# A second array of expert sums that takes odd ranks up to 57 and is read back by accumulating DMAs

## The chip, the core and the metric

The kernel runs on one core of a Trainium2 chip. Its time is the device time of one execution in microseconds (us); the median of several runs is compared. The core has five engines with a queue of instructions each: TensorE (PE, with its weight loads listed apart as PEld), VectorE (DVE), ScalarE (ACT), GpSimd (POOL) and SyncE (SP), which only issues DMAs here. DMAs are carried by 16 DMA engines that all queues share.

## What is computed

One layer of a decoder for 520 tokens (512 of a prompt, 8 samples): a mixer of a state-space branch and dilated attention, a layer norm, and then a mixture of 64 experts, of which each token takes 8. The change touches only the end of the mixture:

```
x  = layer_norm(alpha*x + mixer(x))
acc = zeros(n+1, D);  for each block of tokens of one expert e:
    h  = silu(x[tok] @ w1[e]) * (x[tok] @ w3[e])
    acc[tok] += (h @ w2[e]) * gate
ff  = acc + shared_expert(x)
ple = sigmoid(x @ w_ple_gate) * (p @ w_ple)
x   = layer_norm(alpha*x + ff + ple)
```

All weights are fp32. Every matmul is done as three products of high and low parts.

## The kernel before

After the mixer, `second_phase` norms the residual `x1` (104 tokens on partitions, five tiles of 1024), routes the tokens and sorts the experts by how many tokens they have. The place in that order is the expert's rank, 0 to 63; `CAPS` is the number of rows of each rank, falling from 112 to 56. A loop over `e` from 0 to 64 then works through them: `expert_in(e)` (two products with w1 and w3), `turn(e + 1)` (transposes of the next rank's rows), `expert_out(e - 1)` (the product with w2), `fetch(e + 3)` (token indices of a later rank and the gather of its rows from DRAM on GpSimd's queue). Six weight chunks of 512 KB a rank are loaded by SP and split into high and low parts by ScalarE with VectorE, or with GpSimd for one chunk of six (`lo` at line 265).

`expert_out` scales its rows on ScalarE into `y` (line 1450, two buffers, `YB = 2`) and adds them to a DRAM array of sums with an indirect accumulating DMA, the scatter of line 1451, issued from GpSimd. There are two such arrays, `sumsD[0]` and `sumsD[1]`, zeroed early (line 426). Ranks below `SECOND` = 50 alternate between them; ranks 50 to 61 all go to array 0. Two accumulating DMAs into one array must not overlap, so a scatter waits until the one before it in the same array has landed; GpSimd takes its queue in order and stands while it waits. Also `y` of a rank waits for the landing of the scatter two before, whose buffer it takes. Ranks 62 and 63 do not scatter: their rows stay on chip (`kept`, `last_rows`) and are added by matmuls in `last_norm`.

Beside the experts the loop takes side products from a list: 36 items of the shared expert and of the layer inputs, three that bring the scales of the last norm, and in the kernel before five `second_sums(i)`. An item is due when `(e - 4) * SIDE` reaches its number in the list. `second_sums(i)` loads a tile of array 1 on SP's queue into a buffer (`second`, line 1375) and adds it to `x1[:, i]` on GpSimd (line 1376, recorded at the helper's line 262). After the loop, SP loads the five tiles of array 0 (`acc`, line 1637), GpSimd adds three of them to `x1`, and `last_norm` does the rest: `total(i)` adds the kept rows by matmuls (line 1738 on VectorE), then the norm and the output. A conditional `overflow` (line 1645), not taken here, lies ahead of it.

The order of instructions on each engine is not that of the text: a planner simulates the program at build time, and issues on each engine what is ready in its own simulation, the earlier in the text first.

Of the kernel before, what the change touches and what calls it, by code (L numbers as in the profile page):

```python
# [18 lines left out]
F32 = mybir.dt.float32  # L19
# [4 lines left out]
ALU = mybir.AluOpType  # L24
# [6 lines left out]
TT = 104  # L31
# [16 lines left out]
YB = 2  # L48
PRE = 5
VB = 5  # L50
N_SIDE = 44
SECOND = 50
SIDE = N_SIDE / 55
N_DENSE = 54
assert len(CAPS) == NE

# [144 lines left out]
def trunk_step(ctx: ExitStack, tc: tile.TileContext, I, O):  # L201
    nc = tc.nc
    V, S, G = nc.vector, nc.scalar, nc.gpsimd
# [27 lines left out]
    def open_pool(*a, **k):  # L231
        cm = pool(*a, **k)
        p = cm.__enter__()
        opened.append((p, cm))
        return p

    def close_pool(p):
        at = next(n for n, (q, _) in enumerate(opened) if q is p)
        opened.pop(at)[1].__exit__(None, None, None)
# [21 lines left out]
    def add(e, o, a, b):  # L261
        return e.tensor_tensor(out=o, in0=a, in1=b, op=ALU.add)
# [85 lines left out]
    H, EX = {}, {}  # L348
# [68 lines left out]
    sumsD = [dram.tile([640, 1024], F32, name=f"accD{n}") for n in range(2)]  # L417
# [319 lines left out]
    side = []  # L737
# [357 lines left out]
    R5 = range(5)  # L1095
# [162 lines left out]
    def ffn_turn(hg, m):  # L1258
        ps = bank()
        for k in range(2):  # L1260
            T.transpose(ps[:, m * k:m * k + m], hg[0:m, 128 * k:128 * k + 128], ident[0:m, 0:m])
        hh, hl = (moe.tile([128, 2, MAX_CAP], F32R, tag=nm, bufs=2, name=nm)[:, :, 0:m] for nm in ("hh", "hl"))
        H['turned'] = split(hh, hl, ps[:, 0:2 * m].rearrange("p (k t) -> p k t", k=2))
        return hh, hl
# [9 lines left out]
    def shared_mid(out, hg):  # L1274
        S.activation(hg, out[:, 0:128], AF.Silu)
        mul(V, hg, hg, out[:, 128:256])
        return hg

    def shared_turn(hg, i, c):

        ps = bank()
        T.transpose(ps[:, 0:TT], hg, ident[0:TT, 0:TT])
        split(H['shared'][:, i, 0, c], H['shared'][:, i, 1, c], ps[:, 0:TT])
# [87 lines left out]

    def second_sums(i):

        t = pw.tile([128, 1024], F32, tag="praw", name="second")[0:TT]
        nc.sync.dma_start(t, sumsD[1][TT * i:TT * i + TT])
        add(G, H['x1'][:, i], H['x1'][:, i], t)


    XG, XT, HG, HT, GC, IX = {}, {}, {}, {}, {}, {}
# [3 lines left out]
    def find(e, what=(0, 1)):  # L1383

        m = CAPS[e]
        if e not in OH:
            OH[e] = one_hot(e, m)
        a, b = what[0], what[-1] + 1
        ps = psx.tile([128, 512], F32, tag="x", name="x") if e > 2 else bank()
        for i in R5:  # L1390
            T.matmul(ps[0:m, 3 * a:3 * b], lhsT=OH[e][:, i], rhs=H['what'][:, i, 3 * a:3 * b, e], start=(i == 0), stop=(i == 4))
        both = moe.tile([128, 2], F32, tag="gc", bufs=8, name="both")
        V.tensor_reduce(both[0:m, a:b], ps[0:m, 3 * a:3 * b].rearrange("p (w n) -> p w n", n=3), axis=AX.X, op=ALU.add)
        if 0 in what:
            IX[e] = moe.tile([128, 1], I32, tag="idx", bufs=8, name="idx")
            H['last'] = V.tensor_scalar(IX[e][0:m], both[0:m, 0:1], 1024.0, H['slots'][0:m], op0=ALU.add, op1=ALU.min)  # L1396
        if 1 in what:
            GC[e] = both[:, 1:2]
            if e < NE - 2:
                OH.pop(e)  # L1400
# [7 lines left out]
    def fetch(e):  # L1408
        find(e)
        gather(e)  # L1410

    def gather(e):
        m = CAPS[e]
        G.indirect_dma_start(out=XG[e % 3][0:m], out_offset=None, in_=xD[:, :],  # L1414
                             in_offset=bass.IndirectOffsetOnAxis(ap=IX[e][0:m, 0:1], axis=0),
                             bounds_check=NT - 1, oob_is_err=False)

    def turn(e):
        x, m = XG[e % 3], CAPS[e]
        XT[e] = [moe.tile([128, 8, MAX_CAP], F32R, tag=nm, bufs=2, name=nm)[:, :, 0:m] for nm in ("xgh", "xgl")]  # L1420
        for z in range(2):
            ps = bank()
            for j in range(4):
                k = 4 * z + j
                T.transpose(ps[:, m * j:m * j + m], x[0:m, 128 * k:128 * k + 128], ident[0:m, 0:m])
            src = ps[:, 0:4 * m].rearrange("p (k t) -> p k t", k=4)
            split(XT[e][0][:, 4 * z:4 * z + 4], XT[e][1][:, 4 * z:4 * z + 4], src)

    def expert_in(e):
        ps, m = bank(), CAPS[e]  # L1430
        for q in range(4):
            hi, lo = (t.rearrange("p (k n) -> p k n", k=2) for t in stream.get(AT[e] + q))
            ffn_in(ps[0:m], *XT[e], hi, lo, q, slice(0, m))
        HG[e] = ffn_mid(ps, m)
        XT.pop(e)

    def expert_out(e):
        ps, m = mm2(), CAPS[e]
        hh, hl = HT.pop(e)
        for k in range(2):  # L1440
            hi, lo = stream.get(BT[e] + k)
            for n, (l, w) in enumerate(((hh, hi), (hh, lo), (hl, hi))):
                for h in range(2):
                    T.matmul(ps[0:m, h], lhsT=l[:, k], rhs=w[:, 512 * h:512 * h + 512], start=(k == 0 and n == 0),
                             stop=(k == 1 and n == 2))
        if e >= NE - 2:
            kept(e, ps)
            return
        y = py.tile([MAX_CAP, 1024], F32, tag="y", bufs=YB, name="y")[0:m]
        S.activation(y.rearrange("p (h n) -> p h n", h=2), ps[0:m], AF.Copy, scale=GC.pop(e)[0:m])  # L1450
        G.indirect_dma_start(out=sumsD[e % 2 if e < SECOND else 0][:, :], out_offset=bass.IndirectOffsetOnAxis(ap=IX.pop(e)[0:m, 0:1], axis=0),  # L1451
                             in_=y, in_offset=None, compute_op=ALU.add)
# [24 lines left out]
    def second_phase():  # L1477
# [9 lines left out]
        x1 = H['x1']  # L1487
# [107 lines left out]
        close_pool(disp)  # L1595
        py = open_pool("py")
        side = [(q, i) for q in range(-2, 4) for i in range(-1, 5)]
        side += [(4, -1), (4, 0), (4, 1)] + [(5, i) for i in R5]
        for e in range(NE + 1):
            if e == NE - 1:  # L1600
                last_rows()
            if 0 < e < NE:
                expert_in(e)
            if 0 < e < NE - 1:
                turn(e + 1)
            if e:
                expert_out(e - 1)
            else:
                H['shared'] = py.tile([128, 5, 2, 2, TT], F32R, tag="side", name="st")
                mids = py.tile([MAX_CAP, 1024], F32, tag="y", bufs=YB, name="mids")  # L1610
                mids = [shared_mid(H['first half'][i], mids[0:TT, 128 * i:128 * i + 128]) for i in R5]
            if 0 < e < 6:
                shared_turn(mids[e - 1], e - 1, 0)
            if 0 < e < NE - 1:
                HT[e] = ffn_turn(HG.pop(e), CAPS[e])
            if e + 3 < NE:
                fetch(e + 3)
            if e == 4:
                close_pool(pre)
                pw = open_pool("pw")  # L1620
            while side and (e - 4) * SIDE >= N_SIDE - len(side) + 1:
                q, i = side.pop(0)
                if q == -2:
                    shared_more(i)
                elif q == -1:
                    shared_out(i)
                elif q < 4:
                    layer_inputs(q, i)
                elif q == 5:
                    second_sums(i)  # L1630
                else:
                    last_scales(i)
        assert not side
# [65 lines left out]
    def last_rows():  # L1699

        yy = pw.tile([128, 2, 1024], F32R, tag="pl", name="yy")
        H['yh'], H['yl'] = yy[:, 0], yy[:, 1]
        to = H['to'] = pw.tile([128, 5, TT], F32R, tag="praw", name="to")
        G.memset(yy.bitcast(F32), 0.0)
        G.memset(to.bitcast(F32), 0.0)
        for e in (NE - 2, NE - 1):
            m, z = CAPS[e], 64 * (NE - 1 - e)
            oh = OH.pop(e)
            for tiles in ((0, 1, 2), (3, 4)):
                ps = mm2()[:, 0]  # L1710
                for n, i in enumerate(tiles):
                    T.matmul(ps[z:z + m, TT * n:TT * n + TT], lhsT=oh[:, i], rhs=ident_b[0:TT, 0:TT], start=True, stop=True)
                a, b = tiles[0], tiles[-1] + 1
                S.activation(to[z:z + m, a:b], ps[z:z + m, 0:TT * len(tiles)].rearrange("p (i t) -> p i t", t=TT), AF.Copy)
# [116 lines left out]
    close_pool(gpool)  # L1831
    close_pool(qkv)
    second_phase()


# [16 lines left out]
```

## Time and profile before

| | us |
|---|---|
| median of 3 runs | 1359.04 |
| lowest and highest of them | 1354.28, 1369.57 |
| profiled execution, its own time | 1371.03 |
| span of the profiled execution | 1369.2 |

Over the whole span TensorE is busy 1191.9 us (87%), VectorE 970.3 (71%), ScalarE 700.3 (51%), GpSimd 560.2 (41%). 312.93 MB are moved. The expert loop covers about 480 to 1335 us.

How to read the rows: a time is in us from the start of the span; brackets at the end of a row of a timeline give how long the engine had been idle before it and what the profile takes as the releaser of the wait. Where a releaser had long been done, the wait was for something else, often a DMA. PEclk is the share of TensorE's full clock that was granted; the DMA share is the mean busy share of the 16 DMA engines.

### The profile page before, as it was taken

How to read it: one execution, taken by the hardware profiler on the slowest of the kernel's cores; microseconds unless marked ns; L12 is line 12 of the kernel's file. 1: busy time of each engine (PE TensorE's matmuls, PEld its weight loads, DVE VectorE, ACT ScalarE, POOL GpSimd, SP SyncE). 2: the span in 40 equal slices, each digit the busy share in tenths (PEclk: the TensorE clock that was granted, in tenths of full speed). 3: DMA queues.
4: the chain of work that ended last, by engine and by line, in shares of the span. 5: the costliest groups of instructions: out<-in, count | busy, mean ns of one | idle time of the engine just before them, and what ended most of it. 6: DMA issues, size and time to landing. Idle time of an engine off the chain costs nothing. (4 is left out here: it accounts for less than half of the span.)

```text
span 1369.2 us, 20382 instructions
## 1 busy us (share of the span) xinstructions
PE 1191.9 (87%) x7082; PEld 890.2 (65%) x7084; DVE 970.3 (71%) x1397; ACT 700.3 (51%) x1055; POOL 560.2 (41%) x327
## 2 busy tenths in 40 slices
PE   7699899999997979787899688899999998968783
PEld 7699799999877756565566466576666664434441
DVE  7873748633588877576788578789789777647656
ACT  4131534222213766566567456767567665546562
POOL 1821231010124436243565354465664644464326
PEclk9898899999997989898999899999999999788896
DMA  7476553442512989798899798999999899887773
GB/s 286 134 240 120 191 182 105 118 116 92 191 60 89 294 222 314 226 286 262 257 319 319 224 274 275 310 306 305 303 300 321 288 301 266 224 229 243 260 191 100
DMA packets 114182, 312.93 MB, mean 229 GB/s; under 512 B 36986, under 2 KB 37410, under 8 KB 113000
## 3 DMA queue, kind: packets, MB, share of 16 engines
q1 hardware_dynamic: 68892, 249.24, 54.2%
q0 software_dynamic: 30208, 41.20, 14.0%
q10 hardware_dynamic: 14974, 21.14, 5.9%
q8 instruction: 57, 0.93, 0.3%
q14 instruction: 51, 0.42, 0.1%
HBM read 276.32 MB, written 32.87 MB: 226 GB/s over the span
## 5 line engine op out<-in xcount | busy, mean ns | idle before, releaser
L265 DVE TENSOR_TENSOR lo<-raw,hi 128x1024 fp32r<-128x1024 f32 x371 | 552.6, 1503 | 170.1 <-ACT hi L269 166.0
L269 ACT ACTIVATE hi<-raw 128x1024 fp32r<-128x1024 f32 x434 | 450.9, 1056 | 253.4 <-DMA raw<-in_we_dram 80.0
L1451 POOL DMA_INDIRECT accD<-y,idx x62 | 137.0, 2210 | 267.2 <-ACT hh L269 118.2
L210 PE MATMUL a<-hi,xgh 128*64 128x512 f32 (+18 forms) x512 | 211.8, 414 | 8.8 <-DVE xgl L265 6.0
L210 PE MATMUL a<-lo,xgh 128*64 128x512 f32 (+18 forms) x512 | 210.1, 410 | 7.3 <-DVE lo L265 7.3
L210 PE MATMUL a<-hi,xgl 128*64 128x512 f32 (+18 forms) x512 | 206.9, 404 | 0.0
L265 POOL TENSOR_TENSOR lo<-raw,hi 128x1024 fp32r<-128x1024 f32 x63 | 169.3, 2687 | 46.6 <-ACT hi L269 34.8
L1414 POOL DMA_INDIRECT xg<-xD,idx x64 | 125.0, 1953 | 146.5 <-DVE idx L1396 105.1
L210 PE MATMUL mm<-xh,hi 128*128 128x260 f32 (+1 forms) x576 | 121.7, 293 | 19.1 <-DVE r L259 10.7
L210 PE MATMUL mm<-xl,hi 128*128 128x260 f32 (+1 forms) x576 | 120.2, 291 | 0.8 <-DVE xl L265 0.8
L210 PE MATMUL mm<-xh,lo 128*128 128x260 f32 (+1 forms) x576 | 120.5, 291 | 0.0
L210 PEld LDWEIGHTS a<-hi,xgh 128*64 128x64 f32 (+18 forms) x512 | 75.7, 148 | 53.3 <-DVE xgl L265 7.6
L210 PEld LDWEIGHTS a<-lo,xgh 128*64 128x64 f32 (+18 forms) x512 | 75.6, 148 | 48.4 <-DVE lo L265 11.6
L210 PEld LDWEIGHTS mm<-xh,hi 128*128 128x128 f32 x576 | 92.8, 197 | 20.1 <-issue 11.0
L210 PE MATMUL mm<-lo,hh 128*64 128x512 f32 (+18 forms) x256 | 88.3, 428 | 18.3 <-POOL lo L265 17.8
L210 PEld LDWEIGHTS a<-hi,xgl 128*64 128x64 f32 (+18 forms) x512 | 75.5, 147 | 41.1 <-issue 4.0
L215 PE MATMUL a<-ident,xg 64*128 64x64 f32 (+18 forms) x512 | 57.7, 243 | 46.8 <-DMA xg<-xD,idx 38.5
L215 PEld LDWEIGHTS a<-ident,xg 64*128 64x128 f32 (+18 forms) x512 | 49.6, 148 | 73.0 <-DMA xg<-xD,idx 26.4
L210 PE MATMUL mm<-hi,hh 128*64 128x512 f32 (+18 forms) x256 | 88.0, 425 | 8.8 <-ACT hh L269 8.8
L1450 ACT ACTIVATE y<-mm,both 78x1024 f32<-78x1024 f32 (+19 forms) x62 | 68.8, 1109 | 52.1 <-PE mm L210 35.4
L210 PEld LDWEIGHTS mm<-xl,hi 128*128 128x128 f32 x576 | 92.2, 195 | 1.3 <-DVE xl L265 1.1
L210 PEld LDWEIGHTS mm<-xh,lo 128*128 128x128 f32 x576 | 92.4, 195 | 0.1
(410 smaller groups left out, 1999.1 us busy)
## 6 DMA issues: line engine op xcount, KB each, us to landing
raw<-in_we_dram SPq DMA_DIRECT2D x384, 512.0 KB
raw<-in_wd_dram SPq DMA_DIRECT2D x50, 512.0 KB
accD<-zeros_b POOLq DMA_DIRECT2D x2, 2560.0 KB
praw<-in_wp_dram SPq DMA_DIRECT2D x8, 512.0 KB
base<-in_xtok_dram ACTq DMA_DIRECT2D x1, 2080.0 KB
xD<-base ACTq DMA_DIRECT2D x5, 416.0 KB
second<-accD SPq DMA_DIRECT2D x5, 416.0 KB
acc<-accD SPq DMA_DIRECT2D x5, 416.0 KB
```

What stands on the lines that cost most here:

```text
L210: ins = nc.tensor.matmul(*a, **k)
L215: ins = nc.tensor.transpose(*a, **k)
L265: return e.tensor_tensor(out=o, in0=a, in1=b, op=ALU.subtract)
L269: a = S.activation(hi, src, AF.Copy)
L1414: G.indirect_dma_start(out=XG[e % 3][0:m], out_offset=None, in_=xD[:, :], in_offset=bass.IndirectOffsetOnAxis(ap=IX[e][0:m, 0:1], axis=0), ...
L1450: S.activation(y.rearrange("p (h n) -> p h n", h=2), ps[0:m], AF.Copy, scale=GC.pop(e)[0:m])
L1451: G.indirect_dma_start(out=sumsD[e % 2 if e < SECOND else 0][:, :], out_offset=bass.IndirectOffsetOnAxis(ap=IX.pop(e)[0:m, 0:1], axis=0), ...
```

## The change

Array 1 takes the odd ranks up to 57 (`SECOND` is 58), so ranks 58 to 61 go to array 0 and ranks 50 to 57 alternate. `second_sums(i)` no longer loads and adds: it is one accumulating DMA from array 1 into `x1[:, i]`, on GpSimd's queue. The five are taken out of the side list and stand in the loop, three at `e` = 60 and two at `e` = 61, behind the scatters of ranks 59 and 60 in the text. The side list has 39 items instead of 44, and `SIDE` is 39/52 = 0.75 instead of 44/55 = 0.8.

```
-N_SIDE = 44
-SECOND = 50
-SIDE = N_SIDE / 55
+N_SIDE = 39
+SECOND = 58
+SIDE = N_SIDE / 52
...
     def second_sums(i):
-        t = pw.tile([128, 1024], F32, tag="praw", name="second")[0:TT]
-        nc.sync.dma_start(t, sumsD[1][TT * i:TT * i + TT])
-        add(G, H['x1'][:, i], H['x1'][:, i], t)
+        G.dma_start(H['x1'][:, i], sumsD[1][TT * i:TT * i + TT], accum_op=ALU.add)
...
-        side += [(4, -1), (4, 0), (4, 1)] + [(5, i) for i in R5]
+        side += [(4, -1), (4, 0), (4, 1)]
...
             if e + 3 < NE:
                 fetch(e + 3)
+            for i in {SECOND + 2: (0, 1, 2), SECOND + 3: (3, 4)}.get(e, ()):
+                second_sums(i)
...
-                elif q == 5:
-                    second_sums(i)
```

## Rows read from the trace of the kernel before

**Rows 1.** Windows: length, busy us (count) per engine, PEclk, DMA share, GB/s

```profile
1000.00:1150.00 150.00, 144.14 (x841) 95.15 (x840) 124.01 (x163) 102.57 (x142) 75.84 (x37) 1.00 0.92 296
1150.00:1260.00 110.00, 83.88 (x356) 43.37 (x355) 67.43 (x82) 53.84 (x76) 59.30 (x29) 0.81 0.83 236
1260.00:1330.00 70.00, 58.78 (x244) 29.59 (x243) 45.59 (x49) 41.65 (x59) 24.05 (x12) 0.88 0.76 232
```

**Rows 2.** ScalarE's timeline, y of line 1450: start, us, instruction [idle before <- releaser]

```profile
1008.72 1.11 ACT L1450 ACTIVATE y<-mm,both 68x1024 f32<-68x1024 f32 x1 [0.29 <-PE mm L210]
...
1148.34 1.11 ACT L1450 ACTIVATE y<-mm,both 64x1024 f32<-64x1024 f32 x1 [0.28 <-PE mm L210]
1171.20 1.11 ACT L1450 ACTIVATE y<-mm,both 64x1024 f32<-64x1024 f32 x1 [1.34 <-PE mm L210]
...
1274.03 1.11 ACT L1450 ACTIVATE y<-mm,both 58x1024 f32<-58x1024 f32 x1 [0.89 <-PE mm L210]
1291.69 1.11 ACT L1450 ACTIVATE y<-mm,both 56x1024 f32<-56x1024 f32 x1 [8.36 <-DMA accD<-y,idx]
1308.59 1.11 ACT L1450 ACTIVATE y<-mm,both 56x1024 f32<-56x1024 f32 x1 [5.28 <-DMA accD<-y,idx]
```

**Rows 3.** GpSimd's timeline, scatters of line 1451 for ranks 53 to 61

```profile
1207.62 2.84 POOL L1451 DMA_INDIRECT accD<-y,idx  x1 [4.81 <-ACT hg L1254]
...
1247.77 2.52 POOL L1451 DMA_INDIRECT accD<-y,idx  x1 [4.36 <-DMA accD<-y,idx]
...
1271.65 2.87 POOL L1451 DMA_INDIRECT accD<-y,idx  x1 [0.21 <-issue]
...
1291.91 2.10 POOL L1451 DMA_INDIRECT accD<-y,idx  x1 [10.00 <-DMA raw<-in_we_dram]
...
1308.80 1.43 POOL L1451 DMA_INDIRECT accD<-y,idx  x1 [10.04 <-DMA accD<-y,idx]
...
1324.38 1.70 POOL L1451 DMA_INDIRECT accD<-y,idx  x1 [6.25 <-ACT to L1714]
```

**Rows 4.** The view of line 1451: scatters' landing from 1130 us, sequencer's wait near 1205

```profile
DMA to landing us min/median/max: 16.6/19.0/21.4
...
L1451 POOLq EVENT_SEMAPHORE  x1: 9015/9015/9015, 1197.7 to 1197.7; - x1
```

**Rows 5.** TensorE's and VectorE's timelines: two stalls and an index's wait

```profile
1160.19 0.68 PE L215 MATMUL a<-ident,xg 62*128 62x62 f32 x4 [6.69 <-DMA xg<-xD,idx]
...
1215.51 1.11 PE L210 MATMUL mm<-lo,hh 128*62 128x512 f32 x2 [7.18 <-POOL lo L265]
...
1247.60 0.20 DVE L1396 TENSOR_SCALAR idx<-both,slots 56x1 int32<-56x1 f32 x1 [3.10 <-DMA accD<-y,idx]
```

**Rows 6.** Windows of 10 and 6 us, columns as in the first group

```profile
1160.00:1170.00 10.00, 9.81 (x25) 4.49 (x26) 3.71 (x6) 3.66 (x7) 3.40 (x2) 0.50 1.01 270
...
1324.00:1330.00 6.00, 5.98 (x26) 3.09 (x25) 6.00 (x7) 4.87 (x6) 1.70 (x1) 1.00 0.34 56
1330.00:1336.00 6.00, 4.35 (x18) 1.92 (x16) 3.20 (x4) 3.48 (x4) 2.05 (x1) 1.00 0.75 188
```

**Rows 7.** Tile views: ns min/median/max of the adds and the direct DMAs

```profile
L262 POOL TENSOR_TENSOR base<-base,second x5: 2397/2420/3276, 1161.1 to 1238.7; 104x1024 f32<-104x1024 f32 x5
...
L426 POOL DMA_DIRECT2D accD<-zeros_b x2: 1412/1456/1501, 58.8 to 60.2; - x2
```

**Rows 8.** SP's timeline: the loads of array 0 after the loop

```profile
1329.58 2.09 SPq L1637 DMA_DIRECT2D acc<-accD  x5
```

**Rows 9.** DMA queues of the page: packets, MB, share of 16 engines

```profile
q0 software_dynamic: 30208, 41.20, 14.0%
```

**Rows 10.** The end: GpSimd's adds, VectorE's third total, TensorE's branch

```profile
1333.95 7.00 POOL L262 TENSOR_TENSOR base<-base,acc 104x1024 f32<-104x1024 f32 x3 [7.86 <-DMA acc<-accD]
...
1345.86 1.23 DVE L1738 SCALAR_TENSOR_TENSOR base<-mm,base 104x1024 f32<-104x1024 f32 x1 [5.52 <-PE mm L210]
...
L1645 PEldq COMPARE_BRANCH  x1: 6172/6172/6172, 1337.1 to 1337.1; - x1
```

## Prediction

> **What bounds the kernel now.** I read in this order: the windows view, the times at which the expert results y are written, GpSimd's own timeline, then what stood idle beside it. The windows [rows 1] cut out the stage that the change touches. From 1000 to 1150 us TensorE is busy 144.1 of 150 us at full clock and the transfers fill 0.92 of the time at 296 GB/s. From 1150 to 1260 us TensorE is busy only 83.9 of 110 us, at a granted clock of 0.81, with 236 GB/s; from 1260 to 1330 us 58.8 of 70 us at 0.88, with 232 GB/s. No engine and no transfer is full there, so something waits.
>
> The y rows [rows 2] say how fast the experts go by. Counted back from rank 61, the last that scatters, they are ranks 39, 50, 51, 58, 59 and 60. Ranks 39 to 50 take 1148.34 - 1008.72 = 139.6 us, 12.7 us each. Ranks 50 to 58 take 1274.03 - 1148.34 = 125.7 us, 15.7 us each, although fewer side products are left. Rank 50 is where `SECOND` sends every scatter to array 0, so that each must wait for the one before to land.
>
> GpSimd's timeline [rows 3] shows scatters 53, 55, 57, 58, 59 and 61. Scatter 53 stood 4.8 us, scatter 55 4.4 us, scatters 58 and 59 10.0 us each. The row names a weight load as the releaser of 58, but the y of rank 59 is released by a scatter [rows 2] at 1291.69, 0.2 us before scatter 58 goes: that is the landing of scatter 57, issued at 1271.65, 20.0 us earlier. Likewise 58 lands after 16.9 us (1291.91 to 1308.80). The view of the scatter's line says the same: 16.6 to 21.4 us to landing in this stretch, and one wait of 9.0 us on GpSimd's sequencer, the one ahead of scatter 53 [rows 4]. Where experts could go by in 10 to 13 us, a chain of landings of 17 to 20 us is the bound.
>
> Behind a waiting scatter GpSimd's queue stands: the gathers and every sixth weight split (`lo` on POOL). TensorE then waits 7.2 us for such a split at 1215.51 [rows 5]. One stall has another cause: 6.7 us before 1160.19 for a gathered tile, after which the clock is 0.50 for a slice [rows 5, 6].
>
> **The change, part by part.**
>
> A. Ranks 50 to 57 alternate again. Scatters 51 to 57 wait for the one two before. Upper bound: the stage returns to the pace before it, 125.7 - 8 x 12.7 = 24.1 us. Lower bound: only part of the waits of scatters 53 and 55 reaches TensorE, 4 us of 4.8 + 4.4. The slow step from rank 50 to 51 took 1171.20 - 1148.34 = 22.9 us, 10.2 above the pace, and its stall was a gather's, not a scatter's. I leave it in: 24.1 - 10.2 = **14 us gained**, between 4 and 24.
>
> B. Scatters 58 to 61 still share array 0, but 58 now needs 56, not 57. Its 10.0 us go. The y of rank 59 still waits for 57, whose buffer it takes (`YB` = 2; 8.4 us), so nothing is gained there. The y of rank 60 waited 5.3 us for the landing of 58 [rows 2]; with 58 issued beside 57 that goes. **5 us gained**, between 0 and 10.
>
> C. The five reads. Removed: five SP loads, and five GpSimd adds of 2.42 us at the median and 3.28 at most [rows 7], some 13 us of GpSimd, beside which TensorE had other waits: 0. Added: five DMAs on GpSimd. The trace has no accumulating DMA into SBUF. For the issue the nearest row is the direct DMA of line 426, 1.46 us [rows 7]: five are 7.3 us. Behind them on GpSimd stand a weight split and scatters 59 to 61, and the first of the five must wait for scatter 57 to land, which before the change took 20 us.
>
> For the transfer the nearest row is an accumulating scatter in a quiet stretch: the window from 1324 to 1330 us holds the last scatter and little else, 0.34 x 6 = 2.04 us of all engines for 56 x 6 = 336 KB, 165 GB/s [rows 6]. Five times 426 KB are then 2.13 MB / 165 = 12.9 us. Upper end: scatter 61 needs 1329.58 - 1324.38 = 5.2 us to land [rows 3, 8] with 56 x 4 = 229 KB, 1.86 times as many bytes 9.7 us, five one after another 48 us. Lower end: the plain reads that follow, 188 GB/s at a share of 0.75 [rows 6], that is 251 GB/s and 8.5 us. I take 12.9, an accumulate being nearer to an accumulate.
>
> Is that on the path? All transfers that GpSimd issues are booked on one queue [rows 9], so scatters 59 to 61 come behind these. From scatter 57 to the loads of `acc` (line 1637) it is now 1329.58 - 1271.65 = 57.9 us. In the new order: 58 goes 4 us after 57 and lands in 16.9; 59 lands, with weights still streaming, in another 16.9 where it took about 7; 60 and 61 take 8.5 + 5.2; the five 12.9: 64 us, 6 later. The end has room for part: the adds of `acc` end at 1340.95, and `total(2)`, which needs the last of them, begins at 1345.86, since TensorE's branch at line 1645 takes 6.2 us [rows 10]. That is 4.9 us of cover; without it the whole delay counts. 1 us over it, and half of the 7.3 us of issue as stalls behind the split: **5 us lost**, between 0 and 30.
>
> The Trainium skill speaks against this step: "DMA: Bandwidth & Descriptors", section "SWDGE vs HWDGE vs iDMA", has one queue for all that GpSimd issues, which agrees with [rows 9]. Its section on the anatomy of one DMA has 2.0 us plus bytes at 436 GB/s, an estimate of 2.5 us for scatter 61, where the trace shows 5.2; by that figure the five would move in about 5 us and C would cost 0.
>
> D. The side products are spread to loop 56 instead of 53 (0.75 a loop for 0.8). By loop 50 that is 46 x 0.05 = 2.3 products later. TensorE had 6 us idle from 1000 to 1150 us, while the transfers were at 0.92, so what leaves that stage shortens it little: **1 us gained**, between 0 and 6.
>
> Sum: -14 - 5 + 5 - 1 = **-15 us**. The profiled execution took 1371.0 us (span 1369.2 and 1.8 around it) and would take 1356.0. It lies 12.0 us above the median of 1359.0; the median becomes **1344.0**.
>
> **The rivals.**
>
> *Landings stay the bound.* The y buffers and the index tiles also wait for landings: VectorE stood 3.1 us before the index at 1247.60 for the landing of scatter 54 [rows 5], whatever array it used. If two scatters in flight only land later each, A is 4, B 0, C 1: -4 us, 1355. For it: landings of 17 to 21 us where transfers were at 0.83. Against it: at 0.92 before 1150 us the pace was 12.7.
>
> *The full pace.* A 24, B 10, C 4: about -30, 1329. For it: bytes allow it. Against it: the stall of [rows 5] has its own cause.
>
> *Slower: the reads stand ahead of scatter 58.* GpSimd takes its queue in order, and the adds of before were issued about three ranks ahead of their place in the loop (the first before scatter 51 though written in loop 54). If the five land in the queue before scatter 58, GpSimd waits 20.0 us for 57, issues 7.3 us, and scatter 58 lands 16.9 + 12.9 us later: 57 us after 57's issue, where it was 1308.80 - 1271.65 = 37 [rows 3]. The y of rank 60 comes 20 us later. With A at its lower bound that is +15: 1374. It decides against the change where A is under 20.
>
> **How the numbers follow.** Forecast 0.40, its own range 1337 to 1351; landings stay the bound 0.25; full pace 0.15; reads ahead of scatter 58 0.20. A measurement of this kernel tells about 1% from nothing, 13.6 us: faster is below 1345.4, slower above 1372.6. Five eighths of the forecast and the full pace are faster: 0.25 + 0.15 = 0.40. The rest of the forecast and the second case are within: 0.15 + 0.25 = 0.40. Slower 0.20. The range from 1328 to 1366 leaves out the reads ahead of scatter 58 at their full price and the edge of the full pace, together some 0.2.
>
> **What would show it.** A: y of ranks 50 to 58 in 112 us or less, and no wait of scatters 51 to 57 for a scatter. B: scatter 58 within 6 us of its y. C: issue rows of some 1.5 us for the five, and where they stand: behind scatter 58 by the forecast, ahead of it by the slower rival; the loads of `acc` no more than 5 us later against TensorE's last expert product. The forecast is wrong if the y rows keep 15 us a rank although the scatters go at once, or if GpSimd stands more than 20 us ahead of the five.

## The result and the profile after

The changed kernel takes 1328.85 us (median of 4 runs, 1323.99 to 1338.84), the kernel before beside it 1360.65 us. The ratio is 0.9753, with an interval from 0.9709 to 0.9798; run again later with 6 runs it is 1325.25 us and 0.9737 (0.9700 to 0.9775). So the change brings about 32 us, 36 in the second comparison, where 15 were forecast. Single executions of one kernel differ by 1% and more (the kernel before lay between 1354 and 1372 us), so times are compared by medians and profiles by stretches. The two profiled executions, 1371.03 and 1326.8 us, lie 44 us apart, 12 us more than the medians: a difference of a few us between stretches of single profiles can be chance.

The page of the kernel after begins:

```profile
span 1325.1 us, 20407 instructions
## 1 busy us (share of the span) xinstructions
PE 1188.6 (90%) x7083; PEld 887.7 (67%) x7084; DVE 939.5 (71%) x1397; ACT 700.4 (53%) x1055; POOL 535.2 (40%) x327
```

TensorE is busy as long as before (1188.6 for 1191.9 us), in a span 44 us shorter: what went is idle time. The times at which `y` was written (the rows of [rows 2] read in each profile) say where. In us from the start of the span:

| y of rank | before | after | earlier by |
|---|---|---|---|
| 30 | 893.0 | 885.4 | 7.6 |
| 48 | 1124.0 | 1098.8 | 25.2 |
| 50 | 1148.3 | 1125.5 | 22.8 |
| 58 | 1274.0 | 1227.0 | 47.0 |
| 61 | 1321.0 | 1278.0 | 43.0 |
| end | 1369.2 | 1325.1 | 44.1 |

Half of these 44 us is there before rank 50, where no scatter, array or read differs. Windows of the same ranks (columns as in [rows 1]), ranks 30 to 48, 50 to 58 and 58 to 61, first of before:

```profile
893.00:1124.00 231.00, 219.34 (x1308) 150.58 (x1307) 192.54 (x253) 156.85 (x218) 128.24 (x55) 0.99 0.94 305
1148.30:1274.00 125.70, 98.75 (x423) 50.98 (x423) 81.06 (x98) 64.88 (x90) 68.37 (x33) 0.84 0.84 245
1274.00:1321.00 47.00, 36.64 (x146) 18.29 (x146) 25.53 (x28) 24.41 (x35) 13.51 (x7) 0.82 0.76 228
```

and of after:

```profile
885.40:1098.80 213.40, 208.41 (x1220) 140.11 (x1219) 178.68 (x243) 154.65 (x214) 111.98 (x55) 1.00 1.00 322
...
1125.50:1227.00 101.50, 94.39 (x460) 51.51 (x460) 71.75 (x99) 66.16 (x92) 53.49 (x26) 0.95 0.88 275
1227.00:1278.00 51.00, 37.47 (x146) 17.90 (x146) 27.56 (x28) 26.26 (x36) 16.72 (x11) 0.83 0.85 247
```

In ranks 30 to 48 TensorE works 10.9 us less and idles 5.0 instead of 11.7 us: 17.6 us. In ranks 50 to 58 its idle time falls from 27.0 to 7.1 us and its clock rises from 0.84 to 0.95: 24.2 us. Ranks 58 to 61 are 4 us slower.

GpSimd's timeline shows where the planner put the five reads (L1374) and what stood around them; the scatter line is now L1449. These are scatter 55, scatter 58, the five, the weight split behind them and scatter 59:

```profile
1192.88 1.61 POOL L1449 DMA_INDIRECT accD<-y,idx  x1 [0.20 <-issue]
...
1228.46 2.13 POOL L1449 DMA_INDIRECT accD<-y,idx  x1 [4.05 <-ACT hh L269]
1236.82 4.46 POOL L1374 DMA_DIRECT2D base<-accD  x5 [6.23 <-DMA accD<-y,idx]
1239.77 3.88 POOL L265 TENSOR_TENSOR lo<-raw,hi 128x1024 fp32r<-128x1024 f32 x1
...
1251.69 1.54 POOL L1449 DMA_INDIRECT accD<-y,idx  x1 [8.03 <-PE a L215]
```

Scatters 55 and 58 go as soon as their `y` is there, where they stood 4.4 and 10.0 us in [rows 3]. The five stand behind scatter 58, wait 6.2 us for scatter 57 and need 4.46 us to issue.

### The profile page after: what moved, and what is told of

Its sections match the earlier page's. It is cut to its first block, busy times and chain, and to the rows that moved or that the text cites. A ratio compares the mean times of both kernels' runs of the same rounds, so it can differ in the third digit from the quotient of the medians.

```text
span 1325.1 us, 20407 instructions
## 1 busy us (share of the span) xinstructions
PE 1188.6 (90%) x7083; PEld 887.7 (67%) x7084; DVE 939.5 (71%) x1397; ACT 700.4 (53%) x1055; POOL 535.2 (40%) x327
## 5 line engine op out<-in xcount | busy, mean ns | idle before, releaser
L265 DVE TENSOR_TENSOR lo<-raw,hi 128x1024 fp32r<-128x1024 f32 x371 | 519.1, 1410 | 197.9 <-ACT hi L269 193.2
L1449 POOL DMA_INDIRECT accD<-y,idx x62 | 127.4, 2054 | 283.0 <-ACT hh L269 146.9
L1412 POOL DMA_INDIRECT xg<-xD,idx x64 | 114.1, 1783 | 104.6 <-DVE idx L1394 43.2
L210 PEld LDWEIGHTS a<-lo,xgh 128*64 128x64 f32 (+18 forms) x512 | 76.1, 149 | 45.2 <-DVE lo L265 10.4
L210 PEld LDWEIGHTS mm<-xh,hi 128*128 128x128 f32 x576 | 91.3, 193 | 19.8 <-issue 10.8
L210 PE MATMUL mm<-hi,hl 128*64 128x512 f32 (+18 forms) x256 | 83.6, 409 | 0.0
```

Of the source, the lines that this page charges most:

```text
L210: ins = nc.tensor.matmul(*a, **k)
L265: return e.tensor_tensor(out=o, in0=a, in1=b, op=ALU.subtract)
```

## The experiments

The change has three parts: the spacing of the side items, the arrays, and the form and place of the reads. Two theories stood after the result. Theory N: the arrays carry the gain, and what lies before rank 50 is chance. Theory S, later D1: the spacing carries a good half, since TensorE is full before rank 50. A third, D2, came up with the experiments: the new spacing only makes the planner order the queues better.

| kernel | spacing | arrays to | reads | median us | ratio to before (interval) |
|---|---|---|---|---|---|
| e1_spacing | 0.75 | 50 | load, add, loops 54 to 59 | 1342.45 | 0.9859 (0.9818, 0.9900) |
| e3_old_spacing | 0.8 | 58 | DMA, loops 60, 61 | 1357.98 | 0.9965 (0.9931, 0.9999) |
| e2_load_add | 0.75 | 58 | load, add, loops 60, 61 | 1345.87 | 0.9895 (0.9863, 0.9926) |
| e4_no_reads | 0.75 | 58 | none, array 1 is left out of the sum | 1323.94 | 0.9714 (0.9682, 0.9746) |
| e5_read_only | 0.8 | 50 | DMA, loops 52, 53 | 1379.48 | 1.0120 (1.0051, 1.0189) |
| e6_all_alternate | 0.75 | 62 | DMA, loops 63, 64 | 1325.88 | 0.9725 (0.9659, 0.9790) |
| e9_spacing_071 | 0.709 | 58 | as the change | 1334.51 | 0.9762 (0.9684, 0.9840) |
| e10_later_start | 0.8, 3 loops later | 58 | as the change | 1367.65 | 1.0020 (0.9979, 1.0060) |
| e12_double_full | 0.75, more work | 58 | as the change | 1336.84 | 0.9797 (0.9751, 0.9842) |
| e13_double_late | 0.75, more work | 58 | as the change | 1340.97 | 0.9847 (0.9801, 0.9892) |

### The spacing alone, and everything but the spacing

```
 e1: the kernel before with
-N_SIDE = 44
-SIDE = N_SIDE / 55
+N_SIDE = 39
+SIDE = N_SIDE / 52
+            for i in {54: (0,), 56: (1,), 57: (2,), 58: (3,), 59: (4,)}.get(e, ()):
+                second_sums(i)
 e3: the changed kernel with
-SIDE = N_SIDE / 52
+SIDE = 44 / 55
```

> The kernel before with the new spacing of the 39 side items alone (0.75 a loop); SECOND stays 50, the reads stay load and add in loops 54 to 59. In the changed kernel's profile the y of rank 50 is already 22 us earlier (1126 against 1148 us). Theory S, spacing: the side products that leave the stage before rank 50 give that: 10 to 22 us faster than before, ratio 0.984 to 0.993, and y of rank 50 near 1126 to 1138 us. Theory N: those 22 us are mostly the difference between two executions (the profiled execution of before was 11 us above its median) and of two plans: ratio 0.997 to 1.003, and the pace of ranks 50 to 58 stays near 15 us.

> The changed kernel with the old spacing of 0.8 side items a loop. Theory S: it gives back 10 to 22 us of the 32, ratio to before 0.984 to 0.992. Theory N: it stays where the change is, 0.972 to 0.980. By either theory ranks 50 to 58 keep the pace of 12.6 us a rank.

The spacing alone brings 1.4%, arrays and reads without it 0.35%, both 2.5%. Theory N falls: it had 0.997 or more for e1 and 0.972 to 0.980 for e3. Theory S fits e1, but e3 lies outside its range too (0.984 to 0.992): without the new spacing 28 of the 32 us are lost, more than S gave it, and the gains do not add up. The windows (ranks 30 to 48 and 50 to 58) show both effects apart, e1 first:

```profile
890.00:1104.60 214.60, 208.52 (x1218) 139.72 (x1216) 178.31 (x243) 154.83 (x215) 112.56 (x53) 1.00 1.00 319
1131.30:1245.80 114.50, 97.88 (x461) 52.88 (x459) 75.32 (x99) 65.44 (x93) 68.11 (x32) 0.91 0.88 262
```

and e3:

```profile
889.30:1119.80 230.50, 219.03 (x1313) 150.78 (x1310) 193.25 (x253) 157.03 (x219) 128.71 (x56) 0.99 0.95 306
1144.10:1256.70 112.60, 96.33 (x422) 50.28 (x422) 74.03 (x98) 65.85 (x90) 52.97 (x27) 0.89 0.82 255
```

Ranks 30 to 48 go by the spacing alone: 231.0 and 230.5 us with the old one, 214.6 and 213.4 with the new. Ranks 50 to 58 go by both: 125.7 before, 112.6 with the arrays alone, 114.5 with the spacing alone, 101.5 with both. The profiles put the arrays, with the reads moved out of these ranks, at 13 us with either spacing, but only the 13 us with the new spacing agree with the medians (e1 to the changed kernel: 16.7 us by profiles, 13.6 by medians). With the old spacing the two profiled executions lie 16.4 us apart and the medians 4.3, and 4.8 of the 13 us lie between the `y` of ranks 50 and 51, where both kernels wait for the same gather; so that 13 is not shown. e3 expected 12.6 us a rank and has 14.1.

What the spacing moves is seen in the groups of TensorE by shape (`x<-ph,x1h` is a third of a layer-input product's main part, 8 rows a product; columns: busy us, mean ns | idle), ranks 30 to 48 of before and then of after:

```profile
L210 PE MATMUL x<-ph,x1h 128*104 128x256 f32 x104 | 29.3, 282 | 0.0
```

```profile
L210 PE MATMUL x<-ph,x1h 128*104 128x256 f32 x80 | 22.5, 281 | 0.0
```

104 / 8 = 13 products against 10. ScalarE's `pt` rows, one behind each product, say where the three went. Before, six of the 20 lie ahead of the `y` of rank 30 and one behind that of rank 48; after, seven and three. So two products moved behind rank 48 and one ahead of rank 30.

### What a product costs, and where

```
 e12: which = (2,0), (2,1), (2,2), ranks 38 to 40;  e13: which = (3,2), (3,3), (3,4), ranks 49 to 52
+            for k, l, w, n in [z for _ in range(2 if (q, i) in which else 1) for z in ...]:
```

> The changed kernel, but three layer-input products of the stage where TensorE is full (ranks 38 to 40) are computed twice, the second time over the first. Theory D1: each costs the 5.9 us that a product less gave, so ranks 30 to 48 take about 231 us for 213 and the whole kernel is 15 to 20 us slower than the changed kernel, ratio to before 0.985 to 0.992. Theory D2 (what the new spacing gains is the order of gathers and scatters near rank 50, not TensorE time): TensorE work is hidden under the transfers, less than 8 us, 0.975 to 0.981.

> The changed kernel, but the last three layer-input products (ranks 49 to 52, the ones that the new spacing moved behind rank 48) are computed twice. Theory D1: behind rank 50 TensorE has time to spare, so three products more cost 0 to 8 us, ratio 0.975 to 0.981, clearly less than the same three products before. Theory D2: no difference between this kernel and the one that doubles products of ranks 38 to 40.

For e12, ranks 36 to 45, and beside it the changed kernel's second run:

```profile
957.90:1077.30 119.40, 114.75 (x694) 79.79 (x693) 93.90 (x117) 79.91 (x109) 56.65 (x26) 1.00 0.93 291
```

```profile
953.90:1063.20 109.30, 105.10 (x609) 69.69 (x607) 90.09 (x124) 77.52 (x108) 57.69 (x27) 1.00 0.99 321
```

Three products cost 9.7 us of TensorE and 10.1 us of time: 3.4 us each, paid in full although the transfers are at 0.93 to 0.99. By the size of a product this agrees with the 10.9 us of work that left ranks 30 to 48, 3.6 a product. The 5.9 us that the expectation counted held 6.7 us of idle time too, which went for other reasons. TensorE's waits in ranks 30 to 48, before and then after (columns: us in total, times, longest; the changed kernel has no row for `both`):

```profile
PE mm L210 <- POOL lo L265: 5.9, 3, 2.8
PE x L210 <- DVE both L1393: 3.1, 2, 1.9
```

```profile
PE mm L210 <- POOL lo L265: 2.8, 3, 1.6
```

The median of e12 is 11.6 us above that of the changed kernel in the same comparison, under the 15 expected: its ratio, 0.9797, is one that D2 had forecast (0.975 to 0.981). The stage decides against D2's reason for it, that work of TensorE is hidden under the transfers.

For e13, ranks 48 to 53, and the changed kernel's second run:

```profile
1105.90:1177.80 71.90, 71.90 (x432) 49.45 (x430) 49.72 (x63) 43.16 (x60) 27.65 (x14) 1.00 0.82 250
```

```profile
1100.50:1162.00 61.50, 61.38 (x343) 38.65 (x342) 47.92 (x65) 42.85 (x59) 28.93 (x14) 1.00 0.94 290
```

Here my expectation of 0 to 8 us was wrong: three products more cost 10.4 us here too, and the median rises by 15.7. e12 and e13 are not told apart (0.9751 to 0.9842 and 0.9801 to 0.9892), as D2 had it and D1 had not. The reason is that in the changed kernel both stages are full: here TensorE is busy 61.38 of 61.5 us. With one product in them instead of three, the same five ranks took 76.2 us before (1124.0 to 1200.2) and 64.9 in e3. So the two moved products stand in time in which TensorE had waited, among it the 6.7 us for a gathered tile and the clock of 0.50 after it [rows 5, 6]. That this is why they cost nothing there is argued: no run moved them alone. There is no room for three more.

### Wider still, and later instead of slower

```
 e9:  +SIDE = N_SIDE / 55
 e10: +SIDE = 44 / 55      and   (e - 7) * SIDE   for   (e - 4) * SIDE
```

> The changed kernel with side items spread still wider: 39 items over 55 loops, 0.709 a loop, the last due in loop 59. Theory D1, TensorE is the bound before rank 50 (100% busy from 1100 to 1150 us before): each layer-input product that is left for the ranks after 49 takes its own 5.9 us (231.0 - 213.4 us in ranks 30 to 48 for 13 - 10 products) out of the bound stage, and the stage after has TensorE time to spare. One or two more products leave: y of rank 48 at 1088 to 1094 us, 3 to 10 us faster than the changed kernel, ratio to before 0.968 to 0.973. Theory D2, the new spacing only happens to give a better plan: no trend, anything from 0.970 to 0.995.

> The changed kernel with the old pace of 0.8 side items a loop, but begun three loops later, so that as many items are left at rank 50 as with the new spacing (34.4 due, against 34.5). Theory D1 in the form that what counts is the number of products left after rank 49: y of rank 48 near that of the changed kernel (1099 to 1108 us), ratio to before 0.973 to 0.981. If it is the pace that counts (TensorE is full only from rank 30 on, and this kernel does 13 products there again): ranks 30 to 48 take 228 to 232 us and the gain must show before rank 30 or not at all, ratio 0.985 to 0.997. Theory D2, luck of the plan: no expectation.

e9 is no faster than the change: 0.9762 against 0.9753, where 3 to 10 us were expected. It too has 10 products in ranks 30 to 48, which took 217.9 us; by its `pt` rows five lie ahead of rank 30 and two behind rank 53, so none more left the full stage, and the expectation was not put to the test. Ranks 50 to 58 took 108.1 us. e10 shows that the number of products left is not the whole. In its profile, the fastest of its ten executions (1352.09 us, 15.6 below their median), ranks 30 to 48 took 227.0 us with 11 products, but ranks 48 to 51 took 51.7 us, where the changed kernel has 37.9. The longest wait of TensorE there, 9.5 us, is for a gather; its row on GpSimd, the view of that row (who waited, and the landing) and TensorE's row:

```profile
1121.85 2.17 POOL L1412 DMA_INDIRECT xg<-xD,idx  x1 [0.20 <-issue]
...
  PE a L215: 9.5, 1
...
DMA to landing us min/median/max: 19.2/19.2/19.2
```

```profile
1141.17 0.66 PE L215 MATMUL a<-ident,xg 62*128 62x62 f32 x4 [9.50 <-DMA xg<-xD,idx]
```

GpSimd stood still for only 0.2 us before this gather, but it landed 19.2 us after its issue, where the gather before it needed 8.3 us.

In the kernel before, the gather of the 6.7 us wait [rows 5] stood behind a scatter. It is the one for rank 53. With the old spacing (before, e3, e5) GpSimd issues it behind scatter 49, 16.7 us after the `y` of rank 48 begins; with 0.75 (e1, e2, e4, e6, the changed kernel) ahead of scatter 48, within 0.3 us of that `y`. GpSimd's timeline before and in e1:

```profile
1139.02 1.46 POOL L1451 DMA_INDIRECT accD<-y,idx  x1 [8.03 <-ACT y L1450]
1140.79 1.35 POOL L1414 DMA_INDIRECT xg<-xD,idx  x1 [0.30 <-ACT hi L269]
```

```profile
1104.90 2.92 POOL L1414 DMA_INDIRECT xg<-xD,idx  x1 [1.69 <-PE mm L210]
1108.12 1.48 POOL L1451 DMA_INDIRECT accD<-y,idx  x1 [0.30 <-ACT hh L269]
```

From the `y` of rank 50 to that of 51, windows of before and of e1:

```profile
1148.30:1171.20 22.90, 16.21 (x55) 7.58 (x55) 11.42 (x16) 8.90 (x12) 10.70 (x5) 0.70 1.01 258
```

```profile
1131.32:1142.53 11.21, 11.21 (x61) 6.42 (x59) 8.46 (x13) 7.42 (x12) 3.88 (x2) 1.00 1.03 276
```

This step took 22.9 us before and 18.1 in e3, 11.2 in e1 and 11.1 in the changed kernel. So 7 to 12 us of what the spacing brings in ranks 50 to 58 lie here, and GpSimd's order is what differs, which is D2's mechanism. No run moved this gather alone.

### The reads

```
 e2: the changed kernel with the old body of second_sums
 e4: the changed kernel without
-            for i in {SECOND + 2: (0, 1, 2), SECOND + 3: (3, 4)}.get(e, ()):
-                second_sums(i)
 e5: the changed kernel with  SECOND = 50  and  SIDE = 44 / 55
 e6: the changed kernel with  SECOND = 62  and  {63: (0, 1, 2), 64: (3, 4)}
```

> The changed kernel, but each of the five reads is again a load on SP's queue and an add on GpSimd, in the same loops 60 and 61. If the read in itself brought nothing (my prediction's step C, and the theory that the arrays carry the gain): within 4 us of the changed kernel, ratio to before 0.973 to 0.979. If the accumulating DMA is what makes late reading cheap: the single buffer makes five loads and adds go one after another ahead of the weight loads on SP's queue, 10 to 20 us slower than the changed kernel, 0.983 to 0.991.

> The changed kernel without the five reads: array 1 is never added, so the sums of odd ranks up to 57 are left out of the output. It prices step C. In the changed kernel ranks 58 to 61 took 51 us where 47 were before, with ScalarE waiting for weight loads eleven times. If the reads' 2.13 MB hold up weights and scatters: 5 to 12 us faster than the changed kernel, ratio to before 0.966 to 0.972. If the landings of scatters 58 to 61 set that pace: within 3 us of the changed kernel, 0.973 to 0.978.

> Arrays and spacing of before (SECOND 50, 0.8 a loop), but the five reads are accumulating DMAs in loops 52 and 53. It prices the new read where array 0 is chained. If the read by DMA is the better form by itself (it takes 13 us of adds from GpSimd and five loads from SP): 3 to 8 us faster than before, ratio 0.994 to 0.998. If it is neutral: 0.997 to 1.003. If the five DMAs stand in GpSimd's queue ahead of chained scatters: slower, 1.003 to 1.012.

> The changed kernel with all ranks alternating (SECOND 62) and the five reads in loops 63 and 64, after scatter 61. In the changed kernel ranks 58 to 61 take 51 us, and it goes at 12.6 a rank before. If the chain of scatters 58 to 61 in one array is what makes them slow: 38 to 42 us, but the reads then stand between scatter 61 and the end, about 13 us of transfer beside the loads of the other array: 0 to 8 us slower than the changed kernel, ratio 0.975 to 0.982. If the reads at loop 60 made them slow (theory of step C): ranks 58 to 61 take 42 us as in the kernel without reads, and the end grows from 47 us to 55 to 62.

e2: loads and adds as late as this lose all that the arrays bring (1345.87 us, e1 with the old arrays 1342.45). Ranks 50 to 58 take 101.0 us as in the changed kernel, but from the `y` of rank 61 to the end it takes 69.4 us instead of 47.1: the loads share one buffer, and GpSimd's adds go one at a time, the fifth behind the adds of the other array:

```profile
1255.91 2.34 POOL L262 TENSOR_TENSOR base<-base,second 104x1024 f32<-104x1024 f32 x1 [11.16 <-DMA second<-accD]
...
1297.26 6.93 POOL L262 TENSOR_TENSOR base<-base,acc 104x1024 f32<-104x1024 f32 x3 [2.87 <-DMA acc<-accD]
1305.47 2.34 POOL L262 TENSOR_TENSOR base<-base,second 104x1024 f32<-104x1024 f32 x1 [1.29 <-DMA second<-accD]
```

The accumulating DMA is what makes the late read, and with it the longer use of array 1, pay.

e4 prices the reads: 1323.94 us, 4.9 less than the changed kernel's first median and 1.3 less than its second (1325.25). The intervals of the ratios overlap (0.9682 to 0.9746 and 0.9709 to 0.9798), so the price is not told from nothing. In the profiles it is seen in one stretch, and the waits show by what. ScalarE's waits for weight loads in ranks 58 to 61, with the reads and then without (columns: us in total, times, longest):

```profile
ACT hi L269 <- DMA raw<-in_we_dram: 20.0, 9, 3.1
```

```profile
ACT hi L269 <- DMA raw<-in_we_dram: 9.4, 4, 3.1
```

These ranks take 51.0 us with the reads and 41.9 without, while the chain of scatters 58 to 61 in array 0 is the same. (With the reads in the same place, e9, e12 and e13 took 45.1 to 47.7 us.) e6 agrees from the other side: without the chain and with the reads behind scatter 61, these ranks take 42.2 us, and the end pays instead: GpSimd's adds of `acc` wait for the reads.

```profile
1280.44 4.52 POOL L1374 DMA_DIRECT2D base<-accD  x5 [6.42 <-DMA accD<-y,idx]
1286.43 2.37 POOL L262 TENSOR_TENSOR base<-base,acc 104x1024 f32<-104x1024 f32 x1 [1.47 <-DMA base<-accD]
```

e5: with the old arrays and the old spacing the same five DMAs cost 17.6 us, at the upper edge of its third expectation. They stand before scatter 50, and the next scatter waits for that one to land:

```profile
1141.91 4.51 POOL L1374 DMA_DIRECT2D base<-accD  x5 [1.85 <-DMA accD<-y,idx]
1148.44 1.48 POOL L1449 DMA_INDIRECT accD<-y,idx  x1 [0.30 <-ACT hi L269]
1177.94 1.44 POOL L1449 DMA_INDIRECT accD<-y,idx  x1 [9.43 <-DMA accD<-y,idx]
```

Scatter 50, behind the five, landed after 29.2 us by the view of its line, and its successor went 29.5 us after it. This is the slower rival's mechanism, at another place.

### The changed kernel and the nearest version, side by side

> The changed kernel once more, beside the runs of this call: ratio to before 0.971 to 0.980.

> All ranks alternate and the reads stand behind scatter 61, once more and beside the changed kernel, for a verdict between the two. Ranks 58 to 61 took 42 us instead of 51, the end 49 instead of 47: if that holds, 3 to 8 us faster than the changed kernel, ratio to before 0.968 to 0.974; if the reads cost at the end what they cost in the loop, the same as the changed kernel within 3 us.

1325.25 us (0.9737) and 1326.81 us (0.9726; 0.9686 to 0.9767): no difference that can be told, and not the 3 to 8 us that the shorter ranks 58 to 61 could have given. No version here that does all the work beats the changed kernel.

## Why the prediction was right or wrong

**A held with the new spacing.** 14 us were forecast; between e1 and the changed kernel ranks 50 to 58 are 13 us shorter (114.5 to 101.5), and no scatter from 51 to 57 was released by another scatter. The reads leave these ranks too, and no run parts the two. With the old spacing, as the step was worked out, arrays and reads together bring 4.3 us by medians, so there its size is not confirmed. What the step set aside as a gather's stall (10.2 us) went all the same, by the spacing.

**B and C: the places held, the sizes are less sure.** Scatter 58 went 0.3 us after its `y` was written. The 5 us of B are there in ranks 58 to 61 once the reads are away (47.0 to 41.9, single profiles). C, forecast at 5 us, measures 1.3 to 4.9 by medians, within the noise. The place behind scatter 58 was right, the slower rival's place wrong. The working of C was partly off: issue is 4.46 us, not 7.3, and the price shows as weights that arrive late, not as a later chain of scatters. The loads of `acc`, 4.4 us ahead of the end of TensorE's last expert product before, were 6.0 us ahead after; nothing at the end became later.

**D failed, and with it the size.** The step reads: "TensorE had 6 us idle from 1000 to 1150 us, while the transfers were at 0.92, so what leaves that stage shortens it little". It put 1 us, between 0 and 6; the spacing alone measured 19.8 us (1362.26 to 1342.45). Both rows were right and the conclusion was the wrong way round. TensorE at 144 of 150 us was the bound of that stage: three doubled products added 10.1 us to it in the changed kernel, at transfers of 0.93 to 0.99, and 10.9 us of work that left ranks 30 to 48 went out of their time. The count of 2.3 products later was about right: two moved behind rank 48. But the step gave the stage behind rank 50 no credit for taking them, though its windows [rows 1] show 26 us of idle TensorE, and it did not see that a new spacing has the planner order GpSimd's queue anew: the gather for rank 53 moved ahead of scatter 48, and the step from rank 50 to 51 became 7 to 12 us shorter.

The range from 1328 to 1366 just held the first median, 1328.85, and not the second, 1325.25; the gain is more than twice the one forecast. The *full pace* rival gave 1329, nearly the number, but by luck: it had the arrays worth 24 us and the scatters of the end 10, and nothing more for the spacing.

**What stays open.** With the old spacing, arrays and reads bring 4 us by medians, with the new one 13.6 (e1 to the changed kernel); why is not shown. How much of the spacing's 19.8 us is work that left a full stage and how much is the order of GpSimd's queue is not parted: the profiles show both, and no run changed the place of that gather, or of the products, alone.

## What to carry to other kernels

A stage in which one engine is busy 96% and the transfers read 0.92 has two candidates for its bound, and the idle time left on the engine is no bound on the gain. Doubling a small piece of the engine's work tells: here it cost its whole time, and work taken out paid as well (ranks 30 to 48 in e1: 214.6 us for 231.0). This does not say that taking out more would go on paying; in the changed kernel the transfers of ranks 30 to 48 read 1.00 as well. Ask of each edit that looks like mere bookkeeping how many pieces of work it moves across the border between a full stage and one that waits, and count them in the plan. Where a planner orders the queues, an edit anywhere can also move a gather ahead of or behind a waiting scatter, so a change of one constant should be run with and without the rest. And look up which transfer a wait was for, and how long it took to land: in e10 the gather had been issued without a wait.

## What the runs showed of the hardware

Five direct accumulating DMAs of 426 KB into on-chip memory issue in 4.5 us together on GpSimd; I had expected 7.3. At the quiet end of e6 they landed 5.9 to 14.5 us after their issue. An accumulating scatter of some 230 to 260 KB landed in 5.2 us in a quiet stretch [rows 3, 8], in 16.6 to 21.4 us beside weight loads [rows 4], and in 29.2 us when it was issued behind 2.13 MB of accumulating reads (e5). I had not expected a factor of more than five between the ends. Gathers of some 250 KB landed in 8.3 and 19.2 us within one stretch of e10.
